# Forward substitution of the RWKV-7 chunks: every second head pair on POOL instead of VectorE

## The chip, the cores and the metric

The kernel runs on one core of a Trainium2 chip. The metric is the device time of one execution in microseconds. The core has a matrix engine (TensorE, PE in the profile), three engines for elementwise work (VectorE or DVE, ScalarE or ACT, GpSimd or POOL), a queue engine (SyncE, SP) that here only starts transfers, and 16 DMA engines. Each engine works off its own queue in order and waits on semaphores for the others.

## What is computed

One layer of a hybrid decoder on 512 prompt positions and 8 single-token samples: dilated window attention and RWKV-7 time mixing on the same normalised input, gates, an output projection and a SwiGLU FFN. The part that matters here is the time mixing of the prompt, a recurrence over positions for each of 16 heads with a 64 x 64 state:

```
def step(S, inp):
    r_t, w_t, k_t, v_t, kk_t, a_t = inp
    sa = jnp.einsum('bhij,bhj->bhi', S, -kk_t)
    S = (S * w_t[:, :, None, :] + sa[..., None] * (kk_t * a_t)[:, :, None, :]
         + v_t[..., None] * k_t[:, :, None, :])
    return S, jnp.einsum('bhij,bhj->bhi', S, r_t)

S_last, ys = lax.scan(step, wkv0.astype(jnp.float32), xs)
```

## The kernel before

**Chunks.** The kernel doesn't go through 512 positions one by one. It takes the heads in pairs (NP = 8 pairs, p = 0 to 7) and the positions in NC = 8 chunks of C = 64. Inside a chunk, each position's correction depends on those of the positions ahead of it; that is a triangular system of 64 x 64 for each head and chunk. `pair(p)` prepares the products of a pair (tiles AR, BK, GH, KB, VT), `solve(p)` inverts the triangular matrices that lie in GH, and `chain(p)` carries the state from chunk to chunk: eight rounds of small matmuls on PE into the PSUM tile "ch" (`cbank`, two banks, by the parity of p), scaled by ACT and added up by DVE. Behind it stands a group norm, and the pair's result goes to OB, the input of the projection w_pb. `back(p)` runs solve, turn_a and chain one after another as one side thread of a pair.

**The substitution.** `solve(p)` cuts each 64 x 64 triangle into two diagonal blocks of 32 x 32 and a rest. It moves the diagonal blocks out to memory (TD) and back (LT), so that 128 partitions hold 32 blocks times 4 groups of columns, and inverts all of them at once by forward substitution (lines 1294 to 1304): 31 steps, each a multiplication into a scratch tile t (tag "xt") and an addition into Xs (tile X in the profile), 62 instructions of VectorE that depend on one another. In step s they have m x w elements per partition, m = s // 4 + 1 and w = 31 - s. After every third step (SOLVE = 3) the thread gives way to others. Then X goes through memory again (TE) into GH, and PE joins the blocks. LT and X have SOLVERS = 2 buffers, so the substitutions of two pairs can be under way together; the third waits (flag "x"). The scratch tile "xt" has one buffer, as `Pool.tile` gives unless told otherwise.

**What sets the order.** All work is put out by `Weave.run`: one main thread, `play`, issues the big projections (jobs of 48 matmuls of 260 columns, with the weights split by `wsplit` into a high part by ACT and a low part, wlo, by DVE), and side threads (pair, back, sample_wkv, merge and others) issue theirs when a model of the engines' clocks (`Clocks`, priced by `Unit.price`) says that their inputs are there. The model prices an elementwise instruction of n elements at 0.07 + n / 960 us on DVE and 0.25 + n / 480 us on POOL, so the engine of an instruction changes when the threads behind it go on. A scheduler below orders each engine's queue from this. `more()` picks the next projection: those of the next pair when earlier pairs have let go of their buffers, else one of 16 gate projections ("fill") or of the attention projection. At the end of the recurrence come the w_pb jobs; the first two (n = 0 and 1) are begun with seven of their eight blocks before pair 7's result is there, and finished afterwards. The second uses the "ch" banks.

**POOL** does a few elementwise instructions of each pair (GH and AR scalings at lines 1218 and 1364, the sample state in `sample_wkv`: st and svd) and starts many transfers (the caches kt, oo, fb, bvr, br, OBD and others) in its own queue.

Of the kernel before, what the change touches and what calls it, by code (L numbers as in the profile page):

```python
# [12 lines left out]
ALU = mybir.AluOpType  # L13
# [12 lines left out]
NP = HB // 2  # L26
# [195 lines left out]
def _bc(ap, shape):  # L222
    return ap.to_broadcast(shape)
# [242 lines left out]
def program(tc, I, O):  # L466
    nc = tc.nc
    ck = Clocks()
    V, S, G, SY = (Unit(n, e, tc, ck) for n, e in (("DVE", nc.vector), ("ACT", nc.scalar), ("POOL", nc.gpsimd), ("SP", nc.sync)))
# [4 lines left out]
    wv = Weave(ck, tc)  # L474
    uid = [0]

    def nm(s):
        uid[0] += 1
        return f"{s}_{uid[0]}"

    def pool(name, stack, **kw):
        return Pool(stack.enter_context(tc.tile_pool(name=name, bufs=1, reuse_waits="tile", **kw)), ck)
# [13 lines left out]
    def bank():  # L496
        return axp.tile([128, 512], FP, name=nm("ax"), tag="ax", bufs=3)
# [153 lines left out]
    def full(tag, bufs=1, dt=FP):  # L651
        return ep.tile([128, NT], dt, name=nm(tag), tag=tag, bufs=bufs)
# [621 lines left out]

    def solve(p):
        r2, QI, GH = rw["r2"], rw["QI"], rw["GH", p]
        TD = drp.tile([4, NC, 32, 32], FP, name=nm("TD"))
        TE = drp.tile([4, NC, 32, 32], FP, name=nm("TE"))
        for q in range(4):
            b = q % 2  # L1280
            SY.dma_start(out=TD[q].rearrange("c s t -> s c t"), in_=GH[q // 2][q * 32:q * 32 + 32, :, b * 32:b * 32 + 32])
        if p >= SOLVERS:
            yield from wv.until("x", p - SOLVERS)

        LT = r2.tile([128, 31, 32], FP, name=nm("LT"), tag="LT", bufs=SOLVERS)
        Xs = r2.tile([128, 8, 32], FP, name=nm("X"), tag="X", bufs=SOLVERS)
        V.memset(Xs[:], 0.0)
        for a in range(4):
            V.memset(Xs[a * 32:a * 32 + 32].rearrange("p m t -> p (m t)")[:, a:256:36], 1.0)
        yield (TD,)  # L1290
        for a in range(4):
            SY.dma_start(out=LT[a * 32:a * 32 + 32], in_=TD[:, :, :31].rearrange("q c s t -> (q c) s t"))
        yield (LT,)
        for s in range(31):
            m = s // 4 + 1
            w = 31 - s
            t = r2.tile([128, 128], FP, name=nm("xt"), tag="xt")
            tv = t[:, :m * w].rearrange("p (m w) -> p m w", m=m)
            V.tensor_tensor(out=tv, in0=_bc(Xs[:, :m, s:s + 1], [128, m, w]),
                            in1=_bc(LT[:, s:s + 1, s + 1:], [128, m, w]), op=ALU.mult)  # L1300
            V.tensor_tensor(out=Xs[:, :m, s + 1:], in0=Xs[:, :m, s + 1:], in1=tv, op=ALU.add)
            if s % SOLVE == SOLVE - 1:
                yield (Xs,)
        yield (Xs,)
        te = TE[:].rearrange("q c (j b) t -> (q c) j b t", b=4)
        for a in range(4):
            SY.dma_start(out=te[:, :, a], in_=Xs[a * 32:a * 32 + 32])
        wv.set("x", p)
        yield (TE,)
        for q in range(4):  # L1310
            b = q % 2
            SY.dma_start(out=GH[q // 2][q * 32:q * 32 + 32, :, b * 32:b * 32 + 32], in_=TE[q].rearrange("c j t -> j c t"))
        yield GH
        if p:
            yield from wv.until("at", p - 1)
        T1 = r2.tile([128, NC, 32], FP, name=nm("T1"), tag="AT")
        for h in range(2):
            V.transpose(out=T1[H[h]], in_=GH[h][H[h], :, 0:32])
        yield T1, BANK
        ps = bank()  # L1320
        for c in range(NC):
            for h in range(2):
                a, b = (slice(h * 64 + i, h * 64 + i + 32) for i in (0, 32))
                E.matmul(ps[b, c * 32:c * 32 + 32], lhsT=GH[h][a, c, 32:64], rhs=T1[a, c], start=True, stop=True)
        for h in range(2):
            b = slice(h * 64 + 32, h * 64 + 64)
            S.copy(out=QI[b], in_=ps[b, :256].rearrange("p (c x) -> p c x", c=NC))
        yield QI, BANK
        ps = bank()
        for c in range(NC):  # L1330
            for h in range(2):
                a, b = (slice(h * 64 + i, h * 64 + i + 32) for i in (0, 32))
                E.matmul(ps[a, c * 32:c * 32 + 32], lhsT=QI[b, c], rhs=GH[h][b, c, 32:64], start=True, stop=True)
        for h in range(2):
            a = slice(h * 64, h * 64 + 32)
            S.copy(out=GH[h][a, :, 32:64], in_=ps[a, :256].rearrange("p (c x) -> p c x", c=NC))
        wv.set("solved", p)
        yield GH
# [128 lines left out]
    def back(p):  # L1467
        yield from solve(p)
        yield from wv.until("w0", p)
        yield from turn_a(p)  # L1470
        yield from chain(p)
        if p == NP - 3:
            for i in range(NP - 2):
                yield from wv.until("pair", NP - 1)
                t = full("tmp", 2)
                G.dma_start(out=t[:, :T], in_=OBD[:, i])
                yield (t,)
                o = ob_tile(i)
                split(o[:, 0, :T], o[:, 1, :T], t[:, :T])
                wv.set("ob", i)  # L1480
# [208 lines left out]
    def pb_pre(n):  # L1689
        def pre():  # L1690
            if n == 0:
                yield from wv.until("ob", NP - 3)
                hctx.close()
                mp = mrg["pool"] = pool("mg", mctx, side="right")
                mrg["h"] = mp.tile([128, KD, NT], FR, name="mh")
                mrg["l"] = mp.tile([128, KD, NT], FR, name="ml")
            gb = gp_.tile([128, NT], FP, name=nm("gb"), tag="g", bufs=2)
            ta = full("tmp", 2)
            G.dma_start(out=gb[:], in_=GD[:, KD + n])
            G.dma_start(out=ta[:], in_=TAD[:, n])  # L1700
            mrg[n] = gb, ta
            yield ()
        return pre
# [264 lines left out]
```

## Time and profile before

| | us |
|---|---|
| three runs: median (lowest to highest) | 1312.92 (1310.77 to 1315.44) |
| the profiled execution, its time | 1316.53 |
| the profiled execution, its span | 1314.8 |
| busy: ACT | 610.6 |
| chain that ended last: PE mm | 51% |
| chain that ended last: DVE, all lines | 15% |

The span is the time from the first to the last instruction; the execution's time has 1.7 us more around it. Every instruction of the kernel is recorded at one helper's line (L380), so rows are told apart by their tiles: `xt<-X,LT` is a multiplication of the substitution and `X<-X,xt` an addition. A row of a timeline has the start, the duration, the engine, the operation, what is written from what, and in brackets the idle time ahead of it and who ended it. A row of waits has who waited for whom, the total, the count and the longest.

### The profile page before, as it was taken

The numbers are of one execution on the slowest core, as the hardware profiler recorded it, in microseconds if no ns is written. First come the engines' busy times: TensorE is split into PE (matmuls) and PEld (weight loads), VectorE is DVE, ScalarE is ACT, GpSimd is POOL, SyncE is SP. The second block draws the span as 40 slices with busy tenths as digits, with TensorE's granted clock in tenths as the row PEclk, the third lists the DMA queues.
The fourth block names the chain that finished last, engine by engine and source line by source line (L and its number), as shares of the span: only waits on it lengthen the run. The fifth ranks groups of instructions, "written<-read, shape, count | busy, mean of one in ns | idle before, by whom it ended". The sixth has DMA issues, their size and how long they took to land.

```text
span 1314.8 us, 29468 instructions
## 1 busy us (share of the span) xinstructions
PE 1264.7 (96%) x11738; PEld 1197.5 (91%) x11738; DVE 843.7 (64%) x2221; ACT 610.6 (46%) x1554; POOL 175.0 (13%) x261
## 2 busy tenths in 40 slices
PE   7999999999989989999999999999999999999996
PEld 7998999989978878888888888999999999999996
DVE  6956866954869998886986665555843444332333
ACT  5244244366656656675785665334433232222220
POOL 1300100100223332121123122110200000000000
PEclk9999999999989999997999999999999999999998
DMA  6523654634245554543245454552222222223331
GB/s 215 158 94 96 213 178 146 221 112 172 69 131 136 152 147 141 143 156 97 77 139 168 123 175 157 182 192 85 81 97 97 97 89 89 97 93 89 89 101 65
DMA packets 92137, 169.48 MB, mean 129 GB/s; under 512 B 42416, under 2 KB 47568, under 8 KB 92000
## 3 DMA queue, kind: packets, MB, share of 16 engines
q1 hardware_dynamic: 60880, 102.46, 24.6%
q0 software_dynamic: 14512, 46.47, 11.5%
q10 hardware_dynamic: 16608, 18.68, 4.3%
q8 instruction: 92, 1.51, 0.5%
q14 instruction: 45, 0.37, 0.1%
HBM read 133.20 MB, written 27.94 MB: 123 GB/s over the span
## 4 chain that ended last, share of the span: by engine, by line
PE 64%; DVE 15%; issue 9%; DMA 6%; ACT 4%; POOL 1%; SPq 1%; ACTq 0%; DVEq 0%; POOLq 0%
PE mm L380 51%; PE ax L380 8%; PE ch L380 5%; DVE wlo L380 2%; DVE X L380 1%; DVE xt L380 1%; DMA fb<-FD 1%; DMA sw<-raw 1%; ACT KB L380 1%; DVE k L380 1%; DMA raw<-w_in 1%; SPq L380 1%; DVE raw L380 1%; DVE qk L380 1%; DVE GH L380 1%
## 5 line engine op out<-in xcount | busy, mean ns | idle before, releaser
L380 PE MATMUL mm<-hh,whi 128*128 128x260 f32 x1136 | 340.2, 299 | 0.8 <-ACT gt L380 0.8
L380 PE MATMUL mm<-hh,wlo 128*128 128x260 f32 x1136 | 325.4, 286 | 4.3 <-DVE wlo L380 4.3
L380 PE MATMUL mm<-hl,whi 128*128 128x260 f32 x1136 | 325.7, 287 | 0.0
L380 ACT CAST whi<-raw 128x1024 fp32r<-128x1024 f32 (+1 forms) x165 | 170.1, 1032 | 324.4 <-PE mm L380 290.6
L380 DVE TENSOR_TENSOR wlo<-raw,whi 128x1024 fp32r<-128x1024 f32 (+1 forms) x165 | 197.9, 1199 | 140.2 <-ACT whi L380 137.0
L380 PEld LDWEIGHTS mm<-hh,whi 128*128 128x128 f32 x1136 | 215.7, 190 | 13.3 <-issue 6.0
L380 PEld LDWEIGHTS mm<-hh,wlo 128*128 128x128 f32 x1136 | 215.4, 190 | 6.5 <-DVE wlo L380 5.8
L380 PEld LDWEIGHTS mm<-hl,whi 128*128 128x128 f32 x1136 | 215.5, 190 | 1.4 <-issue 0.2
L380 PE MATMUL mm<-h2l,whi 128*128 128x260 f32 x608 | 171.5, 282 | 0.0
L380 PE MATMUL mm<-h2h,wlo 128*128 128x260 f32 x608 | 171.4, 282 | 0.0
L380 PE MATMUL mm<-h2h,whi 128*128 128x260 f32 x608 | 171.4, 282 | 0.0
L380 PEld LDWEIGHTS mm<-h2h,wlo 128*128 128x128 f32 x608 | 114.5, 188 | 0.0
L380 PEld LDWEIGHTS mm<-h2l,whi 128*128 128x128 f32 x608 | 114.4, 188 | 0.0
L380 PEld LDWEIGHTS mm<-h2h,whi 128*128 128x128 f32 x608 | 114.4, 188 | 0.0
L380 PE MATMUL mm<-fh,wlo 128*128 128x260 f32 x388 | 109.6, 282 | 0.0
L380 PE MATMUL mm<-fh,whi 128*128 128x260 f32 x388 | 109.5, 282 | 0.0
L380 PE MATMUL mm<-fl,whi 128*128 128x260 f32 x388 | 109.5, 282 | 0.0
L380 PEld LDWEIGHTS mm<-fh,whi 128*128 128x128 f32 x388 | 73.1, 188 | 0.0
L380 PEld LDWEIGHTS mm<-fl,whi 128*128 128x128 f32 x388 | 73.0, 188 | 0.0
L380 PEld LDWEIGHTS mm<-fh,wlo 128*128 128x128 f32 x388 | 72.9, 188 | 0.0
L380 DVE TENSOR_TENSOR xt<-X,LT 128x60 f32<-128x60 f32 (+24 forms) x248 | 60.3, 243 | 3.6
L380 DVE TENSOR_TENSOR X<-X,xt 128x60 f32<-128x60 f32 (+24 forms) x248 | 57.6, 232 | 3.8
(390 smaller groups left out, 2588.8 us busy)
## 6 DMA issues: line engine op xcount, KB each, us to landing
raw<-w_in SPq DMA_DIRECT2D x77, 512.0 KB, 3.7
raw<-w_gate SPq DMA_DIRECT2D x22, 512.0 KB, 3.2
raw<-w_up SPq DMA_DIRECT2D x22, 512.0 KB, 3.2
raw<-w_down SPq DMA_DIRECT2D x16, 512.0 KB, 3.5
kt<-kcache POOLq DMA_DIRECT2D x24, 256.0 KB, 3.7
kt<-vcache POOLq DMA_DIRECT2D x24, 256.0 KB, 3.5
sw<-raw ACTq DMA_DIRECT2D x64, 65.0 KB, 3.6
GD<-gt ACTq DMA_DIRECT2D x16, 260.0 KB, 3.0
```

The costliest lines, as they stand in the source:

```text
L380: r = f(*a, **k)
```

## The change

For odd p the two memsets, the multiplications and the additions of the substitution are put on POOL; for even p they stay on VectorE. The main thread waits, ahead of the second w_pb job, until chain(7) has been issued.

```diff
     def solve(p):
         r2, QI, GH = rw["r2"], rw["QI"], rw["GH", p]
+        B = (V, G)[p % 2]
...
-        V.memset(Xs[:], 0.0)
+        B.memset(Xs[:], 0.0)
         for a in range(4):
-            V.memset(Xs[a * 32:a * 32 + 32].rearrange("p m t -> p (m t)")[:, a:256:36], 1.0)
+            B.memset(Xs[a * 32:a * 32 + 32].rearrange("p m t -> p (m t)")[:, a:256:36], 1.0)
...
             t = r2.tile([128, 128], FP, name=nm("xt"), tag="xt")
             tv = t[:, :m * w].rearrange("p (m w) -> p m w", m=m)
-            V.tensor_tensor(out=tv, in0=_bc(Xs[:, :m, s:s + 1], [128, m, w]),
+            B.tensor_tensor(out=tv, in0=_bc(Xs[:, :m, s:s + 1], [128, m, w]),
                             in1=_bc(LT[:, s:s + 1, s + 1:], [128, m, w]), op=ALU.mult)
-            V.tensor_tensor(out=Xs[:, :m, s + 1:], in0=Xs[:, :m, s + 1:], in1=tv, op=ALU.add)
+            B.tensor_tensor(out=Xs[:, :m, s + 1:], in0=Xs[:, :m, s + 1:], in1=tv, op=ALU.add)
...
     def pb_pre(n):
...
+            if n == 1:
+
+                yield from wv.until("chain", NP - 1)
             gb = gp_.tile([128, NT], FP, name=nm("gb"), tag="g", bufs=2)
```

## The prediction

> **What bounds the kernel now.** I read the page first, then busy time by stage, PE's waits, and the timelines of DVE and POOL where the forward substitution runs.
>
> ```profile
> span 1314.8 us, 29468 instructions
> ...
> PE 1264.7 (96%) x11738; PEld 1197.5 (91%) x11738; DVE 843.7 (64%) x2221; ACT 610.6 (46%) x1554; POOL 175.0 (13%) x261
> ...
> DVE  6956866954869998886986665555843444332333
> ...
> L380 DVE TENSOR_TENSOR xt<-X,LT 128x60 f32<-128x60 f32 (+24 forms) x248 | 60.3, 243 | 3.6
> L380 DVE TENSOR_TENSOR X<-X,xt 128x60 f32<-128x60 f32 (+24 forms) x248 | 57.6, 232 | 3.8
> ```
>
> PE is busy for 96% of the span, so nothing counts that doesn't shorten a stop of PE. DVE's 64% is an average: its digits are 8 and 9 from about 375 us, where the substitution starts, and 3 to 5 behind 700 us. The last two rows are the substitution: 496 instructions, 60.3 + 57.6 = 117.9 us of DVE for eight head pairs.
>
> ```profile
> 375.00:475.00 100.00, 91.77 (x822) 84.80 (x821) 94.68 (x285) 53.55 (x130) 33.98 (x45) 0.97 0.51 143
> 475.00:550.00 75.00, 70.45 (x852) 60.74 (x851) 64.80 (x228) 46.46 (x138) 16.68 (x27) 0.98 0.50 146
> 550.00:650.00 100.00, 95.96 (x1035) 85.57 (x1030) 80.03 (x279) 71.20 (x227) 19.27 (x25) 0.91 0.35 107
> 650.00:750.00 100.00, 96.78 (x1169) 85.31 (x1169) 77.94 (x293) 65.74 (x206) 25.34 (x36) 0.98 0.50 145
> 750.00:825.00 75.00, 71.05 (x884) 62.90 (x883) 46.89 (x141) 48.27 (x168) 14.52 (x27) 1.00 0.50 160
> ```
>
> Columns: length, busy PE, weight load, DVE, ACT, POOL, then granted clock and DMA. From 375 to 475 us DVE is the full engine (94.7 of 100 us) and PE loses 8.2 us; over 375 to 825 us PE loses 450 - 426.0 = 24 us. The clock is under 1 in four of five rows. POOL has room in all of them.
>
> ```profile
> PE ch L380 <- ACT GH L380: 4.0, 4, 2.4
> PE mm L380 <- DVE wlo L380: 3.3, 4, 1.4
> PE ax L380 <- DVE sd L380: 3.2, 1, 3.2
> PE ax L380 <- DVE sg L380: 2.7, 1, 2.7
> ...
> PE ax L380 <- DVE X L380: 0.4, 2, 0.3
> ...
> PE ax L380 <- DVE tmp L380: 0.2, 1, 0.2
> ```
>
> These are PE's waits from 375 to 925 us. Eleven of the seventeen rows name DVE, from wlo (3.3) to tmp (0.2), and add up to 15 us. X itself has 0.4 us of them: the substitution is no stop of PE, but DVE's other work is late because the queue in front of it is long. So a shorter DVE queue is worth at most those 15 us and a part of the clock's dips.
>
> **The change part by part.** *Moved.* Pairs 1, 3, 5 and 7 take their substitution to POOL: 4 x 62 = 248 instructions, 117.9 / 2 = 59 us of DVE. Their memsets go too:
>
> ```profile
> L380 DVE MEMSET X<- x40: 65/65/272, 334.8 to 696.0; 32x8 f32 x32, 128x256 f32 x8
> ```
>
> 4 x 0.27 + 16 x 0.065 = 2.1 us, which the wait for the LT transfers hides on either engine. All DMAs of solve stay on SP.
>
> *What one instruction costs on POOL.* No row shows one so small. The nearest:
>
> ```profile
> 513.99 1.04 POOL L380 TENSOR_TENSOR st<-st,sg 128x512 f32<-128x512 f32 x1 [10.06 <-PE ax L380]
> 517.30 0.61 POOL L380 TENSOR_TENSOR svd<-uk,sel 48x256 f32<-48x256 f32 x1 [2.27 <-ACT uk L380]
> ...
> L380 POOL MEMSET sel<- 48x8 f32 x1 | 0.1, 98 | 0.1
> ```
>
> The 31 steps have m x w elements, 1560 in all, 50 on average. The upper end is svd's 0.61 us, the lower end the memset's 0.10. The line through 256 and 512 elements (0.61, 1.04: 1.68 ns an element, 0.18 us fixed) gives 0.26 us at 50, and I take that, as all three have broadcast inputs; with some 0.07 us to the next dependent one (an estimate from the 0.1 us of idle time in front of that memset) a substitution alone takes 62 x 0.33 = 20 us on POOL (ends 6 and 38). On DVE it is 62 x 0.24 = 15 us.
>
> The Trainium skill, page GPSIMD Engine Reference, section Performance versus the Vector engine, speaks against the move: elementwise work with two inputs is about twice as slow there (4497 against 2293 ns at 2048 elements). An estimate by that ratio would be 59 x 1.96 = 116 us on POOL, 29 us for each substitution instead of 20; no run here shows it for such small tiles yet.
>
> *What DVE gives back.* DVE and POOL exclude each other on some instructions:
>
> ```profile
> 394.68 0.94 POOL L380 TENSOR_TENSOR AR<-AR,PC 128x448 f32<-128x448 f32 x1 [0.17 <-PE ax L380]
> 394.74 0.95 DVE L380 TENSOR_TENSOR X<-X,xt 128x54 f32<-128x54 f32 x1
> 468.80 0.20 DVE L380 TENSOR_TENSOR X<-X,xt 128x54 f32<-128x54 f32 x1
> 396.63 2.15 POOL L380 TENSOR_TENSOR GH<-GH,DN 64x512 f32<-64x512 f32 x2 [1.01 <-DVE GH L380]
> 396.59 0.68 DVE L380 TENSOR_TENSOR GH<-ax,wmask 128x512 f32<-128x512 f32 x1
> ```
>
> The same X instruction takes 0.20 us alone and 0.95 us when a POOL tensor_tensor starts just before it: it ends with POOL's (394.68 + 0.94 = 395.62). The GH mask, which reads PSUM (ax), runs at 0.68 us beside POOL. The Trainium skill, page SBUF — State Buffer, section SBUF: two separate sides, states this as an exclusive lock on a port pair that both use, held for the whole instruction; the trace agrees. So 248 x 0.26 = 64 us of POOL work can each stop DVE, or none of it. DVE's busy time without the substitution:
>
> ```profile
> sum 375.00, DVE 120.79; mean DVE 30.20
> ```
>
> That is X and xt alone over the four stages to 750 us, in which DVE is busy for 317.5 us; (317.5 - 120.8) / 375 = 52% is left, some of it reading PSUM, plus the even pairs. With half of the time taken DVE loses 32 us (bounds 0 and 64), and keeps 59 - 32 = 27 us of relief (bounds 59 and -5).
>
> *A wait that the diff doesn't show.* t, tag "xt" (line 1297 before), has one buffer for all pairs. Until now both its users sat on DVE, in order. Now the two substitutions that run side by side are on different engines: the first xt of a POOL group of three steps waits for DVE's last add on it, and the other way round. They do run side by side:
>
> ```profile
> 500.15 0.18 DVE L380 TENSOR_TENSOR xt<-X,LT 128x31 f32<-128x31 f32 x1
> 523.04 0.17 DVE L380 TENSOR_TENSOR X<-X,xt 128x8 f32<-128x8 f32 x1
> 545.82 0.17 DVE L380 TENSOR_TENSOR X<-X,xt 128x8 f32<-128x8 f32 x1
> 714.73 0.19 DVE L380 TENSOR_TENSOR xt<-X,LT 128x31 f32<-128x31 f32 x1
> 727.37 0.17 DVE L380 TENSOR_TENSOR X<-X,xt 128x8 f32<-128x8 f32 x1
> 745.27 0.17 DVE L380 TENSOR_TENSOR X<-X,xt 128x8 f32<-128x8 f32 x1
> ```
>
> Pair 3 starts at 500.15, pair 2 ends at 523.2: 23 us together; pairs 6 and 7 share 714.7 to 727.5, 13 us. Six neighbours overlap so, by 11 to 33 us, about 130 us in all. A group of three steps goes by about every 5 us, so DVE meets some 26 such waits. Behind a waiting xt stand the next wlo (for PE's next weights) and everything else of DVE. Each wait costs 0 where other work was queued in between, up to a whole POOL group, 6 x 0.33 = 2 us, and more if POOL's group itself stands behind a POOL instruction that waits (10.06 us in the st row above). I take 1 us, the middle: 26 us (bounds 0 and 52). This eats the relief: DVE's net is -27 + 26, about nothing.
>
> *POOL's own queue.*
>
> ```profile
> L380 POOL TENSOR_TENSOR svd<-uk,sel 48x256 f32<-48x256 f32 x16 | 10.8, 676 | 41.7 <-ACT uk L380 24.0 <-PE ax L380 17.6
> L380 POOL TENSOR_TENSOR st<-st,sg 128x512 f32<-128x512 f32 x8 | 11.2, 1400 | 32.8 <-PE ax L380 30.6 <-issue 2.1
> ```
>
> These feed PE. They now find substitution steps in front: 0.33 us at least, 2 us for a group. 16 + 8 of them x 0.3 us = 7 us, of which I put half on PE: +3.5 us. The wait for POOL is hardly on PE's list today, so nothing hides the rest for sure.
>
> *The tail.* Pair 7's substitution takes 745.44 - 714.73 = 30.7 us today. On POOL: 20 us alone, some 4 us for DVE's locks, 3 us for hand-offs with pair 6, and waits of POOL's queue, say 6: about 33 us, +2. What the tail can take:
>
> ```profile
> 807.14 0.34 PE L380 MATMUL ch<-GH,KB 128*64 128x64 f32 x4 [2.44 <-ACT GH L380]
> ...
> 812.37 0.67 PE L380 MATMUL ch<-AR 64*64 64x64 f32 x14
> ...
> 828.82 0.41 PE L380 MATMUL ch<-OB,whi 128*128 128x260 f32 x2
> ...
> 833.87 0.40 PE L380 MATMUL mm<-OB,whi 128*128 128x260 f32 x2
> 827.54 0.69 DVE L380 TENSOR_TENSOR OB<-KB,OB 128x512 fp32r<-128x512 f32 x1 [0.69 <-ACT OB L380]
> ```
>
> Pair 7's last half is ready at 828.2 and PE takes it at 833.87, so 5 us of lateness are hidden; but PE already stops in this chain (2.44 us). +1.5 us, bounds 0 and +8.
>
> *The new wait in pb_pre.* The second w_pb job may not be issued before chain(7). In this run chain(7)'s last ch matmuls (812.37) are already ahead of that job's first (828.82), so it costs nothing unless the chain comes 16 us later; then its 5 us of matmuls (828.82 to 833.87) no longer cover, +5 us.
>
> *Sum.* 0 (relief against hand-offs) + 3.5 + 1.5 = +5 us on a run like the profiled one, which took 1316.53 us, 3.6 above the median 1312.92. Against the median: **1318 us**.
>
> **The rivals.**
>
> *Faster: the hand-offs are hidden.* If DVE always has other work queued between two groups, the net relief of 27 us stands. DVE has 317.5 busy us to 750 us, so its queue gets 8% shorter; PE's 15 us of waits for DVE would about halve: -7 us, 1306 us (-15 at the very most: 1298). For it: DVE's queue mixes many kinds of work, and two of the four moved pairs run before 550 us, where DVE is fullest. Against it: the single xt buffer.
>
> *Much slower: POOL's queue stops DVE.* Place: where a group of steps stands behind a POOL instruction that waits for PE (10.06 us) while a DVE xt waits for that group. Price: two such waits of about 7 us for each of four pairs are 56 us of DVE; with a third of it on PE +19 us, 1332 us. It decides from the point where a POOL wait is longer than the work queued on DVE ahead of its next xt, some 3 us. For it: POOL's waits are long because nothing hung on them so far.
>
> *The lock alone.* Were every POOL instruction to hold up DVE for its whole length, the relief would be 59 - 64 = -5 us and the hand-offs would stay: 26 + 5 = 31 us of DVE, a third of it PE's: +10, with the +5 above 1328 us. This is the skill's rule taken at full strength, and the trace bears it out only for instructions with SBUF operands, so it stands at the edge of the forecast.
>
> *No change.* PE's queue is full of other jobs; relief and waits both vanish in it: 1309 to 1317 us.
>
> **How the numbers follow.** What a measurement of this kernel can tell from no change is about 0.3%, 4 us. Forecast, a few us slower (1317 to 1326): 0.27; POOL's queue or the lock at full strength, slower still: 0.19; no change: 0.25; faster: 0.29. So slower 0.46, same 0.25, faster 0.29. The range goes from 1299 (nearly all DVE waits gone) to 1340 (the queue rival with its waits at the long end).
>
> **What would show it.** X and xt of odd pairs on POOL at about 0.26 us where undisturbed; DVE instructions with two SBUF inputs lengthened beside them; idle time of DVE in front of xt ended by POOL; PE's waits for DVE still at 10 us or more; pair 7's substitution at 30 us or more. Wrong if DVE never waits for POOL's X, if PE's waits for DVE fall to half, or if a step on POOL takes 0.6 us: then POOL needs 38 us a pair and the tail grows by more than its 5 us.

## The result and the profile after

| | us |
|---|---|
| before, beside it on the same chip: median (lowest to highest) | 1311.85 (1308.75 to 1315.44) |
| after: median (lowest to highest) | 1358.67 (1357.23 to 1363.05) |
| ratio with its 95% interval | 1.036 (1.033 to 1.040) |
| span of the profiled execution, before and after | 1314.8 and 1361.3 |

The kernel is 47 us slower. The page of after, its busy times, its digits, the chain that ended last by engine, and two groups:

```profile
span 1361.3 us, 29498 instructions
...
PE 1286.6 (95%) x11738; PEld 1214.2 (89%) x11738; DVE 799.8 (59%) x1953; ACT 609.2 (45%) x1554; POOL 264.3 (19%) x529
...
DVE  6957867944797765688575364555764444432234
...
PE 57%; issue 15%; DVE 12%; POOL 8%; DMA 5%; ACT 2%; SPq 1%; DVEq 0%; ACTq 0%; POOLq 0%
...
L380 DVE TENSOR_TENSOR xt<-X,LT 128x60 f32<-128x60 f32 (+24 forms) x124 | 30.5, 246 | 37.1 <-POOL X L380 35.8
L380 POOL TENSOR_TENSOR xt<-X,LT 128x60 f32<-128x60 f32 (+24 forms) x124 | 46.4, 374 | 39.1 <-DVE X L380 21.9
```

DVE has become emptier, as intended (843.7 to 799.8 us), and from about 410 us on none of its digits is above 8. POOL, with 1% of the chain that ended last before, now has 8%. The emptier DVE doesn't help PE: the same 11738 matmuls take longer. Where, is best read by cutting the span in three, the same cuts for both kernels. Columns as in the prediction's table of stages; before, then after:

```profile
0.00:375.00 375.00, 360.70 (x3000) 341.84 (x3001) 260.94 (x649) 188.36 (x496) 47.22 (x76) 1.00 0.47 152
375.00:975.00 600.00, 575.22 (x5985) 527.40 (x5984) 456.02 (x1368) 338.38 (x940) 127.80 (x185) 0.97 0.45 136
975.00:1315.00 340.00, 328.80 (x2757) 328.29 (x2755) 126.72 (x205) 83.85 (x118) 0.00 (x0) 0.98 0.28 91
```

```profile
0.00:375.00 375.00, 358.48 (x2987) 339.36 (x2988) 258.81 (x641) 187.47 (x494) 47.47 (x80) 1.00 0.48 152
375.00:975.00 600.00, 552.61 (x5609) 499.88 (x5608) 380.42 (x1059) 319.56 (x915) 210.01 (x445) 0.94 0.44 129
975.00:1362.00 387.00, 375.46 (x3147) 374.95 (x3145) 160.55 (x254) 102.17 (x148) 6.81 (x4) 0.98 0.29 91
```

Up to 375 us, ahead of the first substitution, little differs. In the 600 us with the substitutions PE gets 376 matmuls fewer done (5985 - 5609). It idles 47.4 instead of 24.8 us (600 less its busy time), and its granted clock is 0.94 instead of 0.97. The work left for behind 975 us is 375.46 - 328.80 = 46.7 us more, which is the loss: it arises in the stage of the recurrence. About half of it is idle time (22.6 us here); the other half is that the same matmuls are busy for 1286.6 - 1264.7 = 21.9 us longer, at the lower clock.

The clock is not a little lower throughout. In the two traces it is either 1 or 0.5, and the stage has 14 stretches at 0.5 after (75 us in all) against 4 before (31 us). All 4, and 10 of the 14, begin during a stop of PE of 0.9 us or more or within 2 us of its end. One of them: a row of PE's timeline, with the stop ahead of it, and two stretches behind it:

```profile
495.65 0.38 PE L380 MATMUL ax<-ident,sg 128*16 128x128 f32 x2 [3.53 <-DVE X L380]
496.50:499.90 3.40, 3.40 (x30) 3.28 (x26) 0.06 (x1) 1.80 (x4) 1.04 (x4) 0.50 0.42 88
500.00:502.00 2.00, 0.87 (x9) 0.60 (x8) 1.83 (x7) 1.70 (x7) 0.36 (x1) 1.00 0.62 96
```

Not every stop has such a stretch behind it (4 of 8 before, 10 of 14 after have one), and no run isolates what brings it on; but a stop of PE can cost more here than its own length. PE's longest waits from 375 to 975 us in after:

```profile
PE ch L380 <- ACT GH L380: 15.6, 3, 7.3
PE ax L380 <- DVE GH L380: 5.1, 3, 3.5
PE mm L380 <- DVE wlo L380: 4.3, 3, 2.2
PE ch L380 <- DVE AR L380: 4.2, 4, 2.4
PE ax L380 <- POOL svd L380: 3.9, 1, 3.9
PE ax L380 <- DVE X L380: 3.5, 1, 3.5
```

The first row names ACT, which is 45% busy. One of its three waits shows how such a row is to be followed back; timelines of POOL, ACT, DVE and PE:

```profile
763.28 0.70 DVE L380 TENSOR_TENSOR OB<-tmp,OB 128x512 fp32r<-128x512 f32 x1
...
772.61 0.20 POOL L380 TENSOR_TENSOR xt<-X,LT 128x8 f32<-128x8 f32 x1
...
773.96 0.22 POOL L380 TENSOR_TENSOR X<-X,xt 128x8 f32<-128x8 f32 x1
774.11 0.55 POOL L380 DMA_DIRECT2D tmp<-OBD  x1
777.98 0.62 ACT L380 CAST OB<-tmp 128x512 fp32r<-128x512 f32 x1 [8.81 <-DMA tmp<-OBD]
778.50 0.62 ACT L380 ACTIVATE GH<-ch,DN 64x64 f32<-64x64 f32 x2
778.63 0.69 DVE L380 TENSOR_TENSOR OB<-tmp,OB 128x512 fp32r<-128x512 f32 x1 [8.58 <-ACT OB L380]
779.18 0.48 PE L380 MATMUL ch<-GH,KB 128*64 128x64 f32 x4 [7.33 <-ACT GH L380]
```

The last step of pair 7's substitution ends on POOL at 774.18. Behind it in POOL's queue stands the start of a transfer, tmp<-OBD, which has nothing to do with pair 7. DVE's last reading of a tmp ahead of it ends at 763.98, so from there on no reader of the tile kept it back: it starts 10.1 us later. (Before, a start of tmp<-OBD at 746.34 comes 0.3 us behind the same addition of DVE, which ends at 746.04.) ACT's queue stands still for 8.81 us until that transfer has landed, and DVE for 8.58 us behind ACT; behind the cast on ACT stands a scaling of the recurrence (GH) that has nothing to do with the transfer, and PE waits 7.33 us for that. The queues pass the wait on, from POOL over ACT to PE, to work that doesn't depend on it.

### The profile page after: what moved, and what is told of

It reads as the page before. It is cut to its first block, busy times and chain, and to the rows that moved or that the text cites. A ratio compares the mean times of both kernels' runs of the same rounds, so it can differ in the third digit from the quotient of the medians.

```text
span 1361.3 us, 29498 instructions
## 1 busy us (share of the span) xinstructions
PE 1286.6 (95%) x11738; PEld 1214.2 (89%) x11738; DVE 799.8 (59%) x1953; ACT 609.2 (45%) x1554; POOL 264.3 (19%) x529
## 4 chain that ended last, share of the span: by engine, by line
PE 57%; issue 15%; DVE 12%; POOL 8%; DMA 5%; ACT 2%; SPq 1%; DVEq 0%; ACTq 0%; POOLq 0%
PE mm L380 46%; PE ax L380 7%; PE ch L380 4%; POOL xt L380 3%; POOL X L380 3%; DVE wlo L380 2%; DMA fb<-FD 1%; DVE X L380 1%; DVE xt L380 1%; POOL kt L380 1%; DMA xt<-xT 1%; DVE GH L380 1%; DVE raw L380 1%; SPq L380 1%; DVE oac L380 0%
## 5 line engine op out<-in xcount | busy, mean ns | idle before, releaser
L380 PE MATMUL mm<-hh,whi 128*128 128x260 f32 x1136 | 343.8, 303 | 0.0
L380 PE MATMUL mm<-hh,wlo 128*128 128x260 f32 x1136 | 330.9, 291 | 7.7 <-DVE wlo L380 7.6
L380 PE MATMUL mm<-hl,whi 128*128 128x260 f32 x1136 | 330.6, 291 | 0.0
L380 DVE TENSOR_TENSOR wlo<-raw,whi 128x1024 fp32r<-128x1024 f32 (+1 forms) x165 | 197.9, 1199 | 147.4 <-ACT whi L380 144.8
L380 PEld LDWEIGHTS mm<-hh,whi 128*128 128x128 f32 x1136 | 219.9, 194 | 11.9 <-issue 5.2
L380 PEld LDWEIGHTS mm<-hh,wlo 128*128 128x128 f32 x1136 | 220.1, 194 | 11.0 <-DVE wlo L380 9.3
L380 PEld LDWEIGHTS mm<-hl,whi 128*128 128x128 f32 x1136 | 220.1, 194 | 1.7 <-issue 0.2
L380 ACT ACTIVATE GH<-ch,DN 64x64 f32<-64x64 f32 x128 | 39.5, 308 | 51.1 <-PE ch L380 41.1
L380 POOL TENSOR_TENSOR xt<-X,LT 128x60 f32<-128x60 f32 (+24 forms) x124 | 46.4, 374 | 39.1 <-DVE X L380 21.9
```

The lines of the kernel that those rows point to most:

```text
L380: r = f(*a, **k)
```

## The experiments

Three things came with the change at once: another order in which the program issues its work (the clock model books the steps on POOL, 0.25 + n / 480 us each), the execution on POOL, and the queues that the scheduler below makes of both. All ratios are against the kernel before on the same chip, with the 95% interval; "odd pairs" means the substitution of pairs 1, 3, 5, 7.

| run | odd pairs on, booked as | else | us | ratio |
|---|---|---|---|---|
| after | POOL, POOL | | 1358.7 | 1.036 (1.033 to 1.040) |
| e2_order_only | DVE, POOL | | 1331.6 | 1.015 (1.011 to 1.018) |
| e3_pool_old_order | POOL, DVE | | 1345.1 | 1.026 (1.021 to 1.031) |
| e4_all_pool | POOL, POOL | even pairs on POOL too | 1499.3 | 1.141 (1.137 to 1.146) |
| e1_own_scratch | POOL, POOL | own scratch | 1373.2 | 1.047 (1.044 to 1.050) |
| e6_state_on_dve | POOL, POOL | st, svd on DVE | 1343.1 | 1.024 (1.021 to 1.027) |
| e7_dma_off_pool | POOL, POOL | transfers on SP | 1338.8 | 1.021 (1.018 to 1.024) |
| e8_pool_cleared | POOL, POOL | both of these | 1329.2 | 1.011 (1.007 to 1.015) |
| e9_cleared_old_order | POOL, DVE | both of these | 1322.8 | 1.009 (1.005 to 1.012) |
| c1_before_cleared | DVE, DVE | both of these | 1304.9 | 0.995 (0.993 to 0.998) |
| e10_cleared_own_scratch | POOL, DVE | both, own scratch | 1336.7 | 1.018 (1.015 to 1.022) |
| e11_only_solve_on_pool | POOL, DVE | as e10, GH and AR on DVE | 1336.8 | 1.018 (1.016 to 1.021) |
| c2_cleared_own_scratch_dve | DVE, DVE | both, own scratch | 1300.9 | 0.990 (0.986 to 0.993) |
| p1_before_pinned | DVE, DVE | held order | 1520.1 | 1.157 (1.152 to 1.161) |
| p2_pool_old_order_pinned | POOL, DVE | held order | 1509.0 | 1.148 (1.144 to 1.152) |
| p5_c2_pinned | DVE, DVE | held order, as c2 | 1523.9 | 1.160 (1.157 to 1.163) |
| p6_e10_pinned | POOL, DVE | held order, as e10 | 1493.8 | 1.137 (1.134 to 1.140) |
| q1_pool_befores_queues | POOL, DVE | queues of before | 1335.0 | 1.016 (1.011 to 1.022) |
| q2_dve_pools_queues | DVE, DVE | queues of e3 | 1334.1 | 1.016 (1.011 to 1.021) |

The times of e1, e2, e4, e8, e9, e10, c1, p1, p2 and p6 lie outside every range that was expected for them (the texts below), so the theories named there cover only a part of what happened.

### The order alone, and POOL alone

e2 books the odd pairs on POOL and lets VectorE execute them; e3 does the reverse.

```diff
+    VP = Unit("POOL", nc.vector, tc, ck)
...
-        B = (V, G)[p % 2]
+        B = (V, VP)[p % 2]
```

```diff
+    GV = Unit("DVE", nc.gpsimd, tc, ck)
...
-        B = (V, G)[p % 2]
+        B = (V, GV)[p % 2]
```

> The changed kernel's order with the old engine: the clock model still books the odd pairs on POOL at POOL's price, but VectorE executes them. Theory O: most of the loss stays, 1335 to 1360 us. Theories H and Q: no engine shares the scratch and POOL's queue is as before, 1306 to 1322 us.

> The odd pairs run on POOL, but the clock model books and prices them as VectorE's. Theory O: close to the kernel before, 1308 to 1325 us. Theories H and Q: the hand-offs and POOL's queue are there as in the changed kernel, 1340 to 1375 us, with 25 us or more of DVE waiting for POOL's X.

The order alone costs 1.45%, 19 us, with every instruction on the engine that it was on before. One thing that it changes is the start of the last pair's recurrence. This is the view of the tile AR from 755 to 840 us, before and then e2; the row has the number of instructions, their shortest, median and longest time in ns, and the first and the last start:

```profile
L380 DVE TENSOR_TENSOR AR<-ax,PC x2: 618/622/625, 759.9 to 773.4; 128x448 f32<-128x448 f32 x2
```

```profile
L380 DVE TENSOR_TENSOR AR<-ax,PC x2: 625/625/625, 755.7 to 797.1; 128x448 f32<-128x448 f32 x2
```

The two rows are the starts of the recurrences of pairs 6 and 7. In e2 pair 6 starts 4 us earlier and pair 7 24 us later (797.1 against 773.4), although the steps have not become slower (a multiplication takes 209 ns in the median, 213 before) and pair 7's substitution ends only 5 us later (750.8 against 745.4). The rest lies behind it: the clock model takes the odd substitutions for later than they are here, and puts other work ahead of what follows them. How this becomes 19 us isn't shown. PE doesn't idle more in e2's profile than before (1329.5 - 1281.0 = 48.5 us against 50.1); it is busy 16.3 us longer, with 8 stretches at half clock in the stage from 375 to 975 us instead of 4.

e3 costs 2.6%, 34 us, in the program's old order, by POOL's execution, by the queues that the scheduler makes of it, or by both; q1 and q2 tell these apart. With the substitution on POOL the new order costs some 14 us (e3's 1345.1 to after's 1358.7), so it costs something on either engine.

### The suspects on POOL: hand-offs and POOL's queue

e1 takes the shared scratch away: the product goes into rows of the pair's own LT that are used up. e4 puts all pairs on POOL.

```diff
-            t = r2.tile([128, 128], FP, name=nm("xt"), tag="xt")
-            tv = t[:, :m * w].rearrange("p (m w) -> p m w", m=m)
+            flat = LT[:].rearrange("p s t -> p (s t)")
+            tv = (flat[:, :m * w] if s else flat[:, 1:32]).rearrange("p (m w) -> p m w", m=m)
```

> The changed kernel, with the multiplication's scratch in dead rows of the pair's own LT, so that the two engines share no buffer. Theory H (hand-offs through the one xt buffer, 35.8 us of DVE waiting for POOL and 21.9 us the other way): DVE no longer waits for POOL's X, and at least half of the 47 us comes back: 1312 to 1335 us. Theory O (the order put out by the clock model, which prices a POOL step at 0.35 us): the order is nearly as before this edit, 1345 to 1365 us. Theory Q (POOL's own queue: transfers and instructions behind the substitution): the waits of ACT and PE for POOL's transfers stay, 1340 to 1360 us.

> All eight pairs on POOL: one scratch buffer, one engine, no hand-off, VectorE relieved of all 118 us. Theory H: faster than the changed kernel, 1312 to 1340 us. Theory Q: POOL carries some 190 us of substitution (0.38 us a step instruction) with its transfers between, slower than the changed kernel, 1365 to 1420 us. Theory O: slower as well, by a later order of all pairs, 1360 to 1400 us.

In e4 every substitution is on one engine again, so that the shared scratch makes no hand-offs there. In e1 the waits of DVE for POOL's X are gone, and it is slower by 14 us than after. PE's longest waits in e1 now stand elsewhere:

```profile
PE ax L380 <- POOL svd L380: 19.1, 3, 8.4
PE ax L380 <- ACT KB L380: 14.5, 2, 13.9
```

The tile svd, which POOL makes for PE, stands behind substitution steps: 19.1 us against 3.9 in after. With all pairs on POOL (e4, from 375 to 1100 us) the kernel loses 14%, and the same row is

```profile
PE ax L380 <- POOL svd L380: 36.2, 5, 10.3
```

That points to POOL's queue. So e6 and e7 clear it from two sides, e8 from both, and c1 does the same to the kernel before:

```diff
+    GS = Unit("POOL", nc.sync, tc, ck)
...
-            G.dma_start(out=OBD[:, p], in_=yf)
+            GS.dma_start(out=OBD[:, p], in_=yf)
...
-        G.tensor_tensor(out=st[:], in0=st[:], in1=_bc(g[:, G_W].unsqueeze(2), [128, NS, 64]), op=ALU.mult)
+        V.tensor_tensor(out=st[:], in0=st[:], in1=_bc(g[:, G_W].unsqueeze(2), [128, NS, 64]), op=ALU.mult)
```

e6 has the st line and the like one of svd; e7 the transfers of 15 lines (bvr, br, OBD, tmp, oo, fb, FD, ms, OAD, st, o_wkvs, ga, TAD), still booked as POOL's.

> The changed kernel, with the sample state's st and svd (24 instructions that PE waits for) back from POOL on VectorE. Theory Q, POOL's in-order queue hurts by these instructions standing behind substitution steps: PE's waits for POOL's svd (3.9 us in the changed kernel, 19.1 with own scratch) go, 1335 to 1350 us. Theory O, the order, and theory T, transfers behind the substitution: 1350 to 1370 us.

> The changed kernel, with the transfers that POOL starts during the substitution and the merge (bvr, br, OBD, tmp, oo, fb, FD, ms, OAD, st, o_wkvs, ga, TAD) started by SP, in the same order. Theory T, that transfers stand behind substitution steps (ACT idle for 8.8 us until a tmp from OBD landed, PE 7.3 us behind it): 1330 to 1348 us. Theories O and Q without transfers: 1350 to 1370 us; over 1370 us if SP's own queue now holds up the weights.

> The changed kernel with both moves (state on VectorE, transfers on SP), in its own order, odd pairs priced as POOL's. If order and queue add up: 18 us (what the order alone cost) above the same kernel in the old order (1322.8), 1333 to 1345 us. If the order costs only where POOL's queue is full: 1318 to 1328 us.

> Control: the kernel before with both moves (state on VectorE, transfers on SP), substitution all on VectorE. All theories: 1308 to 1325 us; VectorE has 24 more instructions, POOL nearly nothing.

Clearing POOL's queue brings after 16, 20 and with both 30 us (1358.7 to 1329.2), and the kernel before only 6 (0.5%). So some 24 of after's 47 us hang on what else stands in POOL's queue, and on the other queues as far as they change with such an edit. In e9 the old order is added to that.

> Both moves of the two runs above, and the odd pairs booked by the clock model as VectorE's (the order of the kernel before). If queue and order together are the whole cost: 1300 to 1322 us, near the control, with DVE's waits for POOL's X still there. If the hand-offs through the one scratch buffer or the slower steps are a cost by themselves: 1330 to 1350 us.

e9 is still 18 us over its control c1 (1322.8 and 1304.9). It is only 6 us under e8, and the intervals of the two ratios overlap: with POOL's queue cleared the order costs little or nothing. The next three run with POOL cleared, the old order and a scratch for each pair, and e11 also with the scalings GH and AR on VectorE, so that POOL has hardly anything but the steps in this stage:

> POOL cleared, old order, and the scratch in the pair's own LT: no hand-off is left. Theory H2 (what remains of the loss, 18 us over the control of 1304.9, is the hand-offs: 31.3 us of DVE idle in front of xt): 1298 to 1310 us, level with the control or better. Rival L (the odd pairs' steps themselves are late on POOL, 0.38 us each and behind GH and AR): 1314 to 1330 us.

> As the run before, with GH and AR scalings (24 instructions, some 26 us) moved from POOL to VectorE: POOL has little but the substitution. H2: as that run, or a few us later for VectorE's extra load. Rival L, by POOL's queue: 5 us or more earlier than that run.

> Control: POOL cleared, substitution on VectorE, scratch in the pair's own LT. All theories: as the first control (1304.9), 1300 to 1312 us, since one engine's queue orders the users of a shared scratch anyway.

Neither hand-offs nor POOL's queue explain this: with no hand-off and little else in the queue, e10 is 36 us over its control c2, twice the gap with hand-offs. GH and AR on POOL make no difference to the time (e11). c2 is the fastest kernel of the study, 1.0% under before.

### Holding the queues

e10 and c2 issue the same program in the same order, but their finished queues on PE are not the same: the scheduler below sorts each queue by a model of its own, and the engine of an instruction is an input to that. The p runs take this freedom away; every engine gets its instructions in the order in which the program issues them.

```diff
-PIN = 0
+PIN = 1
...
-    V, S, G, SY = (Unit(n, e, tc, ck) for n, e in (("DVE", nc.vector), ("ACT", nc.scalar), ("POOL", nc.gpsimd), ("SP", nc.sync)))
+    V, S, G, SY = (Unit(n, e, tc, ck, tc.keep_in_program_order) for n, e in (("DVE", nc.vector), ("ACT", nc.scalar), ("POOL", nc.gpsimd), ("SP", nc.sync)))
```

> The kernel before with every engine's queue held in the order in which the program issues (the scheduler below may move nothing). Control for the next run: no theory hangs on its own time; since the scheduler's moves are meant to fill stops, 1310 to 1400 us.

> The same held order, with the substitution of the odd pairs on POOL (booked and priced as VectorE's, so the program's order is that of the kernel before; PE, ACT and SP have the same queues as in the control). Theory A, the loss of execution on POOL (34 us in the run with the old order) comes from the scheduler below, which makes other queues when the engine changes: within 6 us of the control. Theory B, it comes from POOL itself (its queue stands still behind the steps, the hand-offs, the longer step): 20 to 40 us over the control.

> Kernel before with POOL's transfers and sample state moved away and a scratch of each pair's own (1300.9 us when the scheduler may move), now in held order: control for the next run.

> The same held order with the odd pairs' substitution on POOL (1336.7 us when the scheduler may move, 36 over its control). Neither POOL's queue nor the shared scratch is left to cost anything. Theory A: within 6 us of its control. Theory B with the longer step or the lock as the rest: 20 us or more over its control; pairs' substitution ends late by 5 us each.

Neither theory had this: with the queues of PE, ACT and SP the same, POOL is faster, by 11 us as it is (1520.1 to 1509.0) and by 30 us with its queue cleared and a scratch of its own (1523.9 to 1493.8). The signs are those of plain accounting: relief of VectorE gains, and clearing POOL gains on top of it. So there the longer step on POOL costs nothing that the relief doesn't outweigh. But these kernels are some 200 us longer and PE idles far more in them (188 us in p1's profile), so they don't settle what happens at 1310. The last pair does it there. q1 and q2 carry the list of another kernel's finished queues and chain each engine's instructions in that order; the odd substitutions' own instructions are left free.

```diff
+    for e, q in QUEUES.items():
+        order = [mine[e][k] for a, n in q for k in range(a, a + n)]
...
+        for a, b in zip(order, order[1:]):
+            tc.add_manual_dep(b, a.name, why, reason="hold")
```

> The odd substitutions on POOL as in the run with the old order (1345 us), but PE, ACT and SP have instruction for instruction the queues of the kernel before, and VectorE and POOL theirs without the substitution, which the scheduler puts where it likes. Theory A, the loss of that run is in the queues that the scheduler makes when the engine changes: 1306 to 1320 us. Theory B, POOL's execution itself (its own queue, the hand-offs, the longer step) costs in any order: 1335 us or more. In between: both, and the difference to 1312 is B's part.

> The kernel before, every substitution on VectorE, but PE, ACT and SP have instruction for instruction the queues of the run with the odd substitutions on POOL and the old order (1345 us), VectorE and POOL theirs without the odd substitutions. Theory A: 1335 to 1350 us, for it is the order that costs. Theory B: 1306 to 1320 us.

q1 lies at the lower edge of theory B's range and q2 just under theory A's, so each theory has a part. Together they make a square of four kernels with one issue order:

| | queues of before | queues of e3 |
|---|---|---|
| odd pairs on VectorE | before: 1 | q2: 1.016 (1.011 to 1.021) |
| odd pairs on POOL | q1: 1.016 (1.011 to 1.022) | e3: 1.026 (1.021 to 1.031) |

The queues that the scheduler makes for POOL cost 1.6%, some 21 us, when no instruction of the substitution runs on POOL. POOL's execution costs 1.6% when no queue of PE, ACT and SP has changed. The sum, 3.2%, lies a little over the 2.6% of both, inside the intervals. Queues that were made for one engine need not suit the other, and either figure may hold some of that; the runs don't tell it apart. What POOL's execution costs PE by itself is seen in q1's waits of PE; before has 0.6 us in the first row, 3.2 in the second and 3.3 in the third:

```profile
PE ax L380 <- POOL svd L380: 10.9, 5, 5.4
PE ax L380 <- DVE sd L380: 4.0, 1, 4.0
PE mm L380 <- DVE wlo L380: 3.9, 3, 2.1
```

The longest of the five, with the rows of POOL ahead of it:

```profile
757.98 0.21 POOL L380 TENSOR_TENSOR X<-X,xt 128x8 f32<-128x8 f32 x1
758.14 0.60 POOL L380 TENSOR_TENSOR svd<-uk,sel 48x256 f32<-48x256 f32 x1
758.80 1.22 PE L380 MATMUL ax<-svd,uk 48*128 48x256 f32 x2 [5.43 <-POOL svd L380]
```

svd comes right behind pair 7's last step, and PE stands 5.43 us for it. Its input and its buffer were ready at 750.58 by the trace, and of the 7.56 us from there 5.1 are steps of the substitution. So POOL's queue is 10 of q1's some 20 us directly. The stage from 375 to 975 us in q1:

```profile
375.00:975.00 600.00, 561.63 (x5801) 512.88 (x5800) 406.41 (x1092) 331.57 (x930) 222.59 (x448) 0.95 0.45 132
```

PE idles 38.4 us in it, 13.6 more than before, at a clock of 0.95 instead of 0.97, and 184 matmuls are left over for later.

## Why the prediction was wrong

It forecast 1318 us, with 1299 to 1340; measured were 1358.7. "Slower" had the highest chance (0.46) and came true, but in part by luck: the sum of +5 us came from two small terms, and a large part of the 47 us from something that it had no term for. By its steps:

- **The order, not priced at all.** The prediction counted what each moved instruction costs and left the order of the rest as it was. That is the step that failed first. The issue order alone is worth 19 us on VectorE (e2) and 14 on POOL (e3 to after), the queues made below it another 21 in e3's case (q2). How after's remaining 27 us over e2 divide into queues and execution was measured only for the old issue order; for after's own order it stays open.
- **POOL's own queue, +3.5 us.** Right mechanism, far too small; this is the term that was mis-sized. POOL's execution costs 1.6%, some 20 us, with the other queues held (q1), 10 of them as PE's waits for svd. The prediction put at most one group of steps ahead of svd or st, 2 us, and 0.3 us on average; PE's longest waits for svd are 3.9 us in after, 5.4 in q1, 8.4 in e1 and 10.3 in e4, and transfer starts stand behind the steps too, with ACT, DVE and PE behind those. Clearing the queue brings 30 us in after against 6 in before. A part of that may again be the queues, which can change with such an edit.
- **The rival "POOL's queue stops DVE"** (1332 us) had the mechanism, but put the damage on DVE's xt. DVE's waits in front of xt did come (35.8 us), but PE's large waits are for svd and for ACT behind a transfer.
- **Hand-offs, 26 us of DVE.** Measured 35.8 us in 18 waits of up to 3.5 us, so rather well sized. That they decide the time isn't shown: taking them away made the kernel 14 us slower twice (e1, e10), in kernels whose queues changed with it; in held order cleared queue and own scratch together gain 15 us on POOL (1509.0 to 1493.8), 19 against the controls. Their own effect stays open.
- **The lock, 32 us of DVE.** Wrong side. The single durations of DVE's instructions other than the substitution add up to 836.7 us before and 839.3 after: 3 us. (They are added one by one; where rows overlap, the busy time counts once.) The largest group, from which before had a mean of 1199 ns too:

```profile
L380 DVE TENSOR_TENSOR wlo<-raw,whi 128x1024 fp32r<-128x1024 f32 (+1 forms) x165 | 197.9, 1199 | 147.4 <-ACT whi L380 144.8
```

  It is POOL that waits (last section).
- **Steps on POOL, 0.26 us and 0.33 from one to the next.** Measured 0.29 to 0.30 in the median, and 0.37 to 0.40 from one to the next. The tile xt on both engines in after, and three steps of POOL's timeline:

```profile
L380 DVE TENSOR_TENSOR xt<-X,LT x124: 141/212/1071, 385.6 to 753.5; 128x60 f32<-128x60 f32 x12, 128x28 f32<-128x28 f32 x8, 128x54 f32<-128x54 f32 x8, 128x48 f32<-128x48 f32 x8
L380 POOL TENSOR_TENSOR xt<-X,LT x124: 202/294/2189, 413.3 to 772.6; 128x60 f32<-128x60 f32 x12, 128x28 f32<-128x28 f32 x8, 128x54 f32<-128x54 f32 x8, 128x48 f32<-128x48 f32 x8
759.99 0.30 POOL L380 TENSOR_TENSOR xt<-X,LT 128x64 f32<-128x64 f32 x1
760.36 0.32 POOL L380 TENSOR_TENSOR X<-X,xt 128x64 f32<-128x64 f32 x1
760.76 0.32 POOL L380 TENSOR_TENSOR xt<-X,LT 128x75 f32<-128x75 f32 x1
```

  62 steps of 0.38 us are 23.6 us instead of 20. The ratio of the medians is 294 / 212 = 1.4. The Trainium skill, page GPSIMD Engine Reference, section Performance versus the Vector engine, has about 2; for these small tiles the measurement decides.
- **The tail, +1.5 us.** The substitution itself was sized well: pair 7's takes 33.9 us in after (740.3 to 774.2), where 33 were forecast. But its recurrence starts at 829.16 instead of 773.4 us, 56 us later (DVE's timeline of after):

```profile
829.16 0.62 DVE L380 TENSOR_TENSOR AR<-ax,PC 128x448 f32<-128x448 f32 x1 [1.57 <-PE ax L380]
```

  The price was worked out as if the pair started when it did before, and as if its recurrence followed at once. The substitution starts 25.5 us later, and from its end to the recurrence pass 55 us instead of 28; in e2, without POOL, 46. The longer step alone doesn't make the odd pairs late: from their first step to their last they take 87, 36, 36 and 34 us in after, and 72, 46, 61 and 31 before.
- **Relief of DVE, 27 us.** Its busy time fell by 44 us, more than the sum had; but PE's waits for wlo stayed (3.3 to 4.3 us), and all its waits for DVE from 375 to 975 us rose from 15 to 23 us. So they hung on something other than how full DVE is. The prediction read its digits roughly, too: behind 700 us there are 6s and an 8 as well, not only 3 to 5.
- **The wait in pb_pre at nothing.** The kernel before with this wait alone has the same queue on every engine, and so has after without it: it costs nothing. This was right.

## What to carry to other kernels

Before work is moved to an emptier engine, list what else stands in that engine's queue and who waits for it: its share of busy time doesn't show that, and one transfer start behind a row of small dependent steps can stop three other engines. Where a planner or a scheduler sets the order from the engines, an edit can change every queue, and here that was worth 14 to 21 us at each of two levels; compare under the same queues before a cause is named. The fastest kernel found doesn't move the substitution at all: it clears POOL's queue and gives each pair its own scratch, on VectorE (1300.9 us, ratio 0.990, 0.986 to 0.993).

## What the runs showed of the hardware

The lock between POOL and VectorE falls mostly on the side with the short instructions. Timelines of POOL and of DVE in after:

```profile
423.03 1.23 POOL L380 TENSOR_TENSOR xt<-X,LT 128x54 f32<-128x54 f32 x1
424.34 0.30 POOL L380 TENSOR_TENSOR X<-X,xt 128x54 f32<-128x54 f32 x1
422.91 1.21 DVE L380 TENSOR_TENSOR wlo<-raw,whi 128x1024 fp32r<-128x1024 f32 x1
```

A step that takes 0.30 us alone takes 1.23 beside wlo, which started 0.12 us ahead of it, and ends behind it; wlo keeps its 1.21 us (its mean before is 1.20). Of the 248 steps on POOL 32 take more than 0.45 us, 28.2 us together, where 32 undisturbed ones would be 32 x 0.30 = 9.6. The Trainium skill, page SBUF — State Buffer, section SBUF: two separate sides, has it that whichever starts first holds the ports for its whole instruction and the other is blocked; the trace agrees. Of the 32, nearly all begin beside an instruction of DVE that started before them, and end 0.1 to 0.2 us behind it. With instructions of mostly 0.7 to 1.2 us on DVE and 0.3 on POOL, the short one is here the one that finds the ports taken.

Most of a small step on POOL doesn't depend on its size: 0.20 us for 128x8 (at 772.61) and 0.32 for 128x75 (at 760.76), nine times as much. Between two dependent steps lie 0.07 to 0.08 us (759.99 + 0.30 to 760.36, 760.36 + 0.32 to 760.76).
